# A gated attention block on one core: norm factors in x, sums of products in PSUM, merges and two gates among the units

## The chip, the core and the metric

One core of a Trainium2 chip runs the whole program once. The metric is the device time of one execution in microseconds (us). The engines are TensorE (PE: products, with PEld for loading its weights), VectorE (DVE), ScalarE (ACT), GpSimd (POOL) and SyncE (SP), whose queue issues the DMA transfers. Each engine takes its instructions strictly in the order in which the program lists them, and waits on semaphores for the others. SBUF is the working memory of the engines; PSUM, in eight banks of 128 x 512 numbers, takes the results of PE.

## The reference

x is 2048 tokens by 1024. In short:

```
h = rms_norm(x) * norm_gain
proj = h @ w_in                     # 1024 x 8448
q, k, v of A (8 heads, 2 kv heads), q, k, v of B (3 groups of 8 heads), ga, gb (512 each), mg (2 x 1024)
ya = windowed attention of A * silu(ga)
yb = softmax-merge over the 3 groups of the dilated attentions of B * silu(gb)
merged = sigmoid(mg0 + b0) * (ya @ w_branch_a) + sigmoid(mg1 + b1) * (yb @ w_branch_b)
out = x + merged @ w_out
```

q and k get a norm per head, and both branches a relative-position bias.

## The kernel before

Every float32 operand of a product is split into a high and a low float16 part, and a product is three: high with high, low with high, high with low. The weights are scaled by a power of two first, found from their sum of squares.

**Prologue.** Sixteen tiles of x (128 tokens) are loaded (x_load, line 437), squared on ACT for the norm (x_square), scaled by the norm factor on DVE (x_scale, 471), turned by PE (x_turn, 475) and split into XH and XL (x_hi, x_lo), which stay in SBUF. The gain of the norm is not in x: it is multiplied into every weight tile on POOL (gains, 182; w_gain, 187; g_gain, 334) ahead of the square (w_square, 220) that the scale comes from (w_sum, 230, a product with ones on PE, line 199; w_pow on DVE). Once four tiles of x are there, PE computes the silu gates of chunks 0 and 1 of 128 columns directly (g_step, 368): 24 products of 512 columns for each quarter of the tokens.

**Units.** Fourteen units (unit_order, 48): A0, B of head pair 0 with dilation 4, A1, then the others of B. Each unit has eight steps; a step projects two blocks of 128 tokens (Pair, 641: 48 products of 384 columns, line 657) while the attention of earlier blocks goes on (Item, 773): logits on PE (825), bias and maximum on DVE (860), exponents and split on ACT and DVE (868, 873, 877), a transposing DMA of p (883), the values (894), and a store to DRAM (zd for B, za for A). An A unit has 32 such items, a B unit 16. The order of all instructions is written out as a plan: `at(t, f)` puts f at time t, in steps, into a heap, and the lists in capitals at the top hold the offsets. Between the products of the units stand other pieces of work: loads and scales of the next unit's weights, and the squares of weights of later stages. A dictionary `fill` lists gates that are computed directly within given steps; before, it holds only pair 0 (mg_step, 1117), in four steps of two gates behind the last unit.

**Gate stage.** The other gates come in pairs of 128 columns each (PAIRS, 62; "m" for merge gates, "s" for silu gates). Pair 1 is computed directly for two quarters of the tokens (gate_pair, 1363). Then come halves (gate_group, 1423): a block product of 2 x 2 blocks in seven instead of eight products (the scheme of Strassen and Winograd), each of twelve matmuls (line 1441). It needs sums of blocks of x (x_sums, 1398: POOL adds on line 1406, DVE on 410 and 1413, ACT on 1409; four chunks for each of two halves of the tokens) and sums of weights (w_sums, 1086: POOL 1109, ACT 1110, DVE 1104). Each of the seven products has a PSUM bank of its own (`fps`, eight banks); ACT copies (1446), DVE additions (1449) and POOL additions (1452) join them; then come tanh on ACT (1350, 1359), for silu a product on DVE (1360), and a store to DRAM. In 19 halves each pair's weights are prepared (prep, 1371) while the pair ahead is computed.

In the same stage lie the merges: eight of A (a_merge, 977) and sixteen of B (b_merge_q, 1011), each for one quarter of the tokens. A merge loads what the units stored, forms the factors of the softmax in small DVE and ACT operations (988 to 1000; 1026 to 1039), multiplies on POOL (1005; 1043) and, for B, adds on DVE (1047, 1048). Its result, y, goes straight into a YPart (921): four transposes by PE (939), the product with the silu gate (942), a maximum (946) and a store to ytd; after the fourth quarter a sum over the partitions by PE (max2, 959, the matmul on line 199).

**Branch and output stages.** The products of y with the branch weights (branch_pair, 1592, line 320) are gated, merged on POOL, split again and multiplied by w_out (group, 1671, line 1667).

Of the kernel before, what the change touches and what calls it, by code (L numbers as in the profile page):

```python
# [40 lines left out]
SX = 2.0 ** 10  # L41
# [21 lines left out]
PAIRS[2:2], PAIRS[0:0] = [("s", 4), ("s", 6)], [("s", 2)]  # L63

V_ONES = 0.077
EVAC = (0.015, 0.025, 0.099)
NORM = (0.028, 0.136, 0.32, 0.626, 0.744, 0.904, 0.962, 1.033, 1.118)
LS = 2.887
LAGS = {'A': (-0.21, 0.002, 0.019, 0.144, 0.276, 0.337, 0.417), 'B': (-0.156, -0.001, 0.042, 0.169, 0.19, 0.379, 0.525)}
LV = {'A': 1.111, 'B': 1.829}  # L70
OUT = 0.007
DRAIN = 0.8
A_MERGE = (4.588, 5.306, 7.494, 7.578, 10.432, 1.944)
B_MERGE = (4.5, 5.692, 7.721, 9.584, 10.41, 10.858, 13.0, 2.546)
Y_PART = (-4.492, 1.142, 1.179, 2.058, 2.995)
GATE = (-0.1, -0.064, 0.329)
W_STEP = (0.1, 0.465, 1.9, 0.445, 4.197, 0.146, 0.342)
W_MAX = (3.762, 3.892)
N_PREP = (5.9, 6.3, 7.15, 7.753)
B_GAP = (0.25, 0.138, 0.231)  # L80
W_LAST = 1.9
T_SUM = (3.065, 4.03)
Y_MAX = (1.0, 3.749, 2.734)
X_SQ = (5.098, 1.401, 9.779, 2.051)
X_CH = (9.3, 2.65, 1.024, 0.955, 1.155, 1.305)
X_ST = (1.3, 0.179)
X_G = (7.5, 15.282, 45.87)
X_GP = (2.1, 5.694, 7.094, 7.694, 8.894, 10.194)
# [3 lines left out]
T_Y = (2.0, 0.8, 1.897, 1.5, 4.347, 26.0, 0.5, 1.3, 2.282, 1.289, 2.066)  # L92
T_P = (3.726, 15.7, 4.2, 8.277, 5.649)
T_X = (0.5, 25.538, 5.083)
T_Z = (66.0, 8.5, 10.8, 11.961, 4.431)
T_O = (0.5, 11.195, 25.513, 29.616, 59.0, 67.057)
T_G = (-54.762, -17.359, -13.9, -13.5)
T_S = (0.0, 0.0, 1.45, 1.512, 1.132, 2.442, 1.723, 1.505, 0.8, 1.857)
T_H = (-20.666, 0.693, 0.178)
T_GATE = (0.1, -0.19, 0.735, 1.0, 2.8)  # L100
T_W = (5.5, 1.621, 8.634, 1.493, 15.16, 15.823, 0.472, 0.8, 1.345)
T_B = (20.984, 6.5, 1.55, 0.725)
T_BR = (7.513, 0.071, 21.94, 8.769, 39.063)
T_A = (0.3, 0.262, 1.5, 0.8, 1.2)
T_M = (16.0, 14.0, 2.0, 2.0, 1.097)
# [11 lines left out]
def block_kernel(tc, x, w_units, w_gate, w_mrg, w_brn, w_out, w_bra, gain, qkg, sink, bias_a, bias_b, b_merge, out):  # L117
# [34 lines left out]
    gn = cst.tile([128, NCH], F32, name="gn")  # L152
# [28 lines left out]

    def gains(raw, c0, n):

        v = raw[:, c0:c0 + 2, :n]
        G.tensor_tensor(v, v, gn[:, c0:c0 + 2].unsqueeze(2).to_broadcast([128, 2, n]), OP.mult)  # L185

    def w_gain(u, i):
        gains(wtiles[u][0], 2 * i, 384 if u < NU else 256)

# [1610 lines left out]
```

## Time and profile before

| | |
|---|---|
| median of three runs | 2061.72 us (2061.12 to 2063.66) |
| profiled execution | 2062.36 us |
| its span, first to last instruction | 2060.6 us |
| mean granted PE clock | 0.982 |
| busy: PE, DVE, ACT, POOL | 1922.8, 1488.7, 1099.2, 1084.6 us |

Busy times are of the whole span and hide that stages have different limits. So they are to be read by stretches: the prediction cuts the span where PE's products change from one line of the kernel to the next. A row of such a view names the stretch, its length, then for each engine its busy time with the number of instructions, the granted clock of PE (1.00 is full speed), the mean share of time in which the sixteen DMA engines were busy, and GB/s. Rows of waits name the instruction that waited, what released it, and total, number and longest of the waits in us. Rows of one line give minimum, median and maximum duration in ns.

### The profile page before, as it was taken

The page shows a single profiled execution, that of the slowest core. Times are in us where ns is not written, and L with a number is a line of the kernel's source. Part 1 is how long each engine was busy: PE and PEld are TensorE (multiplying, and loading weights), DVE is VectorE, ACT ScalarE, POOL GpSimd, SP SyncE. Part 2 cuts the span into 40 slices and gives each one's busy share as a digit, 9 for nine tenths or more (in the row PEclk, how much of TensorE's full clock was granted, in tenths as well). Part 3 has the DMA queues.
Part 4 walks back from the last instruction along what each step waited for, and adds up shares of the span by engine and source line. Part 5 has one row for each costly group of instructions (what it writes and reads, how often), then busy time and mean ns, then how long its engine had stood idle before and what let it go on. Part 6 is the DMA issues. An engine that isn't in the chain of part 4 may idle for free. (4 is left out here: it accounts for less than half of the span.)

```text
span 2060.6 us, 40879 instructions
## 1 busy us (share of the span) xinstructions
PE 1922.8 (93%) x13700; PEld 1202.9 (58%) x13700; DVE 1488.7 (72%) x3478; ACT 1099.2 (53%) x2493; POOL 1084.6 (53%) x2460
## 2 busy tenths in 40 slices
PE   8989999999999999999999997778889899999999
PEld 5566666786678667876788653233344444434444
DVE  6588769867677677667776657978888877787522
ACT  7477668766666666666666653353333335442200
POOL 4254565556656656656665636755566541123434
PEclk9999999999999999999999999889999999999999
DMA  5269779975876786866775661145556555779764
GB/s 228 81 116 198 128 155 159 196 142 112 173 151 121 142 164 116 165 143 122 156 149 100 122 146 62 46 160 178 162 166 191 168 174 162 234 227 283 238 233 154
DMA packets 625460, 325.71 MB, mean 158 GB/s; under 512 B 462688, under 2 KB 565472, under 8 KB 623968
## 3 DMA queue, kind: packets, MB, share of 16 engines
q1 hardware_dynamic: 625248, 323.10, 64.8%
q8 instruction: 107, 1.75, 0.4%
q14 instruction: 105, 0.86, 0.2%
HBM read 138.56 MB, written 73.92 MB: 103 GB/s over the span
## 5 line engine op out<-in xcount | busy, mean ns | idle before, releaser
L657 PE MATMUL pj<-wh,XH 128*128 128x384 f16 x1792 | 585.2, 327 | 3.6 <-DVE vt L697 3.4
L657 PE MATMUL pj<-wh,XL 128*128 128x384 f16 x1792 | 586.5, 327 | 0.0
L657 PE MATMUL pj<-wl,XH 128*128 128x384 f16 x1792 | 585.0, 326 | 0.0
L657 PEld LDWEIGHTS <-XH 128*128 128x128 f16 x3584 | 411.9, 116 | 148.1 <-issue 5.8
L868 ACT ACTIVATE pr<-pr,z 128x256 f32<-128x256 f32 (+3 forms) x512 | 226.2, 494 | 37.2 <-DVE z L860 37.0
L657 PEld LDWEIGHTS <-XL 128*128 128x128 f16 x1792 | 207.5, 116 | 64.2 <-issue 0.3
L860 DVE CUSTOM_DVE_ANT_0 pr<-s,b,ubuf 128x256 f32<-128x256 f32 (+3 forms) x512 | 218.4, 463 | 30.2 <-PE s L825 27.6
L721 DVE TENSOR_TENSOR rw<-rw,qr 128x512 f32<-128x512 f32 (+1 forms) x112 | 112.2, 1002 | 141.1 <-POOL vt L684 118.9
L877 DVE SCALAR_TENSOR_TENSOR p<-pr,p 128x512 f16<-128x512 f32 (+2 forms) x256 | 185.6, 725 | 24.9 <-ACT p L873 22.4
L728 POOL TENSOR_TENSOR rw<-rw,g 128x128 f32<-128x128 f32 (+1 forms) x224 | 149.0, 684 | 90.0 <-DVE rw L721 84.8
L743 POOL COPY spl<-spl 128x256 f16<-128x256 f16 (+1 forms) x224 | 85.5, 411 | 169.9 <-DVE spl L738 168.5
L873 ACT ACTIVATE p<-pr 128x512 f16<-128x512 f32 (+2 forms) x256 | 159.5, 623 | 25.1 <-DMA pt<-p 16.7
L734 ACT ACTIVATE spl<-rw 128x512 f16<-128x512 f32 (+1 forms) x112 | 72.1, 644 | 185.9 <-POOL vt L684 162.8
L825 PE MATMUL s<-kq 128*128 128x256 f16 (+3 forms) x1328 | 149.6, 243 | 21.6 <-DMA kq<-spl 16.3
L281 POOL TENSOR_TENSOR rs_t<-rs_y 128x8 f32<-128x8 f32 (+2 forms) x345 | 91.1, 264 | 143.6 <-DVE rs_y L272 119.2
L320 PE MATMUL fps<-Y,wh 128*128 128x512 f16 x512 | 154.2, 382 | 6.8 <-DVE kp L1600 3.6
L894 PEld LDWEIGHTS <-pt 128*128 128x128 f16 x3024 | 124.1, 97 | 49.7 <-DMA pt<-p 22.2
L894 PE MATMUL pv<-vt,pt 128*128 128x65 f16 (+1 forms) x2784 | 132.0, 193 | 15.3 <-DMA pt<-p 15.2
L1667 PE MATMUL fps<-wt,M 128*128 128x512 f16 (+1 forms) x684 | 145.2, 375 | 0.0
L825 PEld LDWEIGHTS <-kq 128*128 128x128 f16 x1328 | 109.8, 98 | 59.5 <-DMA kq<-spl 17.4
L185 POOL TENSOR_TENSOR wraw<-wraw,gn 128x768 f32<-128x768 f32 (+1 forms) x100 | 136.6, 1374 | 0.3 <-DMA wraw<-in_w_mrg_dram 0.3
L1441 PEld LDWEIGHTS <-wh 128*128 128x128 f16 x760 | 76.9, 102 | 91.2 <-issue 11.0
(226 smaller groups left out, 3799.5 us busy)
## 6 DMA issues: line engine op xcount, KB each, us to landing
wraw<-in_w_units_dram SPq DMA_DIRECT2D x56, 384.0 KB, 4.4
mgd<-fg SPq DMA_DIRECT2D x64, 256.0 KB, 2.4
mtd<-mm SPq DMA_DIRECT2D x56, 256.0 KB, 3.2
M<-mtd SPq DMA_DIRECT2D x8, 1792.0 KB, 9.5
zd<-z SPq DMA_DIRECT2D x192, 66.0 KB, 1.9
Y<-zd SPq DMA_DIRECT2D x48, 264.0 KB, 4.2
wraw<-in_w_mrg_dram SPq DMA_DIRECT2D x44, 256.0 KB, 4.0
xt<-in_x_dram SPq DMA_DIRECT2D x16, 512.0 KB, 8.8
```

Of the source, the lines that this page charges most:

```text
L185: G.tensor_tensor(v, v, gn[:, c0:c0 + 2].unsqueeze(2).to_broadcast([128, 2, n]), OP.mult)
L320: out.append(lambda w=w, xx=xx, ch=ch, i=i: T.matmul(ps[:], lhsT=w[:, ch, c0:c0 + 128], rhs=xx[:, ch, ts], start=(i == 0), stop=(i == n - 1)))
L657: out.append(lambda lhs=lhs, rhs=rhs, ch=ch, k=k: T.matmul(ps[:, :384], lhsT=lhs[:, ch, :], rhs=rhs[:, ch, :384], start=(k == 0), stop=(k ...
L721: V.tensor_tensor(q, q, self.rr[:, :n].unsqueeze(2).to_broadcast([128, n, HD]), OP.mult)
L728: G.tensor_tensor(q[:, i, :un.nq, :], q[:, i, :un.nq, :], g, OP.mult)
L825: T.matmul(self.sv[j][:, o:o + w], lhsT=q[0][:, h, q[1]:q[1] + 128], rhs=kt[:, kh + v * un.nk, k0:k0 + w], start=(v == 0), stop=(v == 1))
L860: V.tensor_tensor_reduce(out=self.pv[:, j, self.p0:self.p0 + W], in0=self.sv[j], in1=un.bias[:, self.h0 + j, self.b0:self.b0 + W], scale=I ...
L868: A.activation(v, v, AF.Exp, bias=self.stat(j), scale=-1.0)
L873: A.activation(self.sp[:, :128 * n], self.pr, AF.Copy, scale=PSC)
L877: V.scalar_tensor_tensor(self.sp[:, 128 * n:], self.pr, PSC, self.sp[:, :128 * n], OP.mult, OP.subtract)
L894: T.matmul(self.po[:, j, :w], lhsT=p[:, n * j + s, :], rhs=un.v[key][:, vh, c0:c0 + w], start=(k == 0 and s == 0), stop=(k == 2 and s == n ...
L1667: mm.append(lambda ch=ch, k=k, w=w, i=i: T.matmul(ps[:, :cols.stop - cols.start], lhsT=m[:, a, ch, k, :], rhs=wt[w][:, b, ch, cols], start ...
```

## The change

Four things change together.

1. The gain of the norm is loaded once, broadcast to 128 partitions (gr), scaled by a power of two (gain_scale), and multiplied into x by x_scale, which becomes an operation on two tensors. All POOL multiplications of weights by the gain are removed; the constant scale SX becomes a value found at run time (sx, isx, ihx).
2. A half of a pair keeps its seven products in three PSUM banks: U1 = A11 B11 is copied out, S2 T2 is added on top of it in the same bank, which is copied out again, then S3 T3 and A22 N4; S4 B22 is added on top of S1 T1. The sums of x lose their factor of a quarter, and the POOL additions go. The last gate reads its sum from PSUM.
3. The merges of A and of B's head pairs 0 to 2 move into the units, at steps 25.4 to 31 and 33.1 to 39 (A), and from steps 44.8, 68.8 and 92.8 on (B). They use a buffer of their own (zz, one copy) and store y to DRAM (yd) by two transfers for each chunk. The YParts stay in the gate stage, 7.12 us apart, and load y from there. Pair 3 of B is merged in the gate stage as before.
4. The list of pairs loses the silu pair of chunks 2 and 3. These two chunks are computed directly, one gate in each of steps 1, 3, 5, 7 (in A0) and 17, 19, 21, 23 (in A1). The merge pair of chunk 3 takes the direct place behind the units. The gate stage has 17 halves.

The many other constants are offsets of the plan. The core of the diff:

```diff
-SX = 2.0 ** 10
+SX = 2.0 ** 9
...
-PAIRS[2:2], PAIRS[0:0] = [("s", 4), ("s", 6)], [("s", 2)]
-
...
+MERGES = (25.362, 1.5, 33.1, 1.639, 44.848, 2.916)
...
+A_MERGE = (0.705, 0.964, 0.937, 0.95, 1.1, 1.13, 0.986)
+B_MERGE = (0.5, 0.65, 0.712, 0.456, 1.15, 1.031, 1.725, 1.5, 1.879)
+Y_PART = (-4.658, 1.142, 1.254, 2.446, 2.904)
+A_FILL = ((1, 3, 5, 7), (17, 19, 21, 23))
+X_GAIN = 6.588
-T_Z = (66.0, 8.5, 10.8, 11.961, 4.431)
+T_Z = (52.0, 7.12, 13.638, 4.085, 5.0)
...
-    def gains(raw, c0, n):
-
-        v = raw[:, c0:c0 + 2, :n]
-        G.tensor_tensor(v, v, gn[:, c0:c0 + 2].unsqueeze(2).to_broadcast([128, 2, n]), OP.mult)
-
-    def w_gain(u, i):
-        gains(wtiles[u][0], 2 * i, 384 if u < NU else 256)
...
+    gr = sp0.tile([128, D], F32, name="gr")
+
+    def gain_scale():
+        m = sm.tile([128, 1], F32, name="gm")
+        V.tensor_reduce(m[:], gr[:], AX.X, OP.max, apply_absolute_value=True)
+        s, i = pow2(m[:], "x")
+        V.tensor_scalar(sx[:], s[:], SX * 2.0 ** -15, None, OP.mult)
+        V.tensor_scalar(isx[:], i[:], 2.0 ** 15 / SX, None, OP.mult)
+        V.tensor_scalar(ihx[:], isx[:], 0.5, None, OP.mult)
+        V.tensor_scalar(gr[:], gr[:], s[:], 2.0 ** -15, OP.mult, OP.mult)
+        done.add("gain")
...
-        V.tensor_scalar(xts[t][:], xts[t][:], xss[groups[t]][:, i:i + 1], None, OP.mult)
+        assert "gain" in done and ("sq", t) in done
+        V.scalar_tensor_tensor(xts[t][:], xts[t][:], xss[groups[t]][:, i:i + 1], gr[:], OP.mult, OP.mult)
...
+    at(X_G[0] + X_GP[5] + .1, g_load, 2)
+    for c in range(3):
         b = X_G[c]
-        chain([(b + X_GP[0] * i, g_gain, c, i) for i in range(2)]
-              + [(b + d, f, c) for d, f in zip(X_GP[1:], (g_square, g_sum, g_pow, g_hi, g_lo))])
+        chain(in_turn(b, X_GP[1:], [(f, c) for f in (g_square, g_sum, g_pow, g_hi, g_lo)]))
     at(X_W[0], w_load, 0)
...
-        def __init__(self, chunk, q, y, o):
-            self.chunk, self.q, self.y, self.o = chunk, q, y, o
+        def __init__(self, chunk, q):
+            self.chunk, self.q = chunk, q
         def load(self):
-            assert ("gt", self.chunk, self.q) in done
-            nc.sync.dma_start(out=self.o, in_=gtd[self.chunk][:, 512 * self.q:512 * self.q + 512])
+            c, q = self.chunk, self.q
+            assert ("gt", c, q) in done and ("yd", c, q) in done
+            self.y, self.o = spare(), spare()
+            nc.sync.dma_start(out=self.y.rearrange("p (b f) -> p b f", b=4),
+                              in_=yd[c][512 * q:512 * q + 512, :].rearrange("(b p) f -> p b f", p=128))
+            nc.sync.dma_start(out=self.o, in_=gtd[c][:, 512 * q:512 * q + 512])
         def plan(self, t):
...
+    def y_keep(c, q, v):
+        d = yd[c][512 * q:512 * q + 512, :].rearrange("(b p) (h e) -> p b h e", p=128, h=2)
+        for h in range(2):
+            nc.sync.dma_start(out=d[:, :, h, :], in_=v[:, :, h, :])
+        done.add(("yd", c, q))
+
     def a_merge(t, j, q):
-        nhalf[0] += 1
...
         def product(c):
-            y = spare().rearrange("p (b h e) -> p b h e", b=4, e=HD)
             hs = slice(2 * c, 2 * c + 2)
-            G.tensor_tensor(y, z[:, :, hs, 0:HD], e1[:, :, hs].unsqueeze(3).to_broadcast([128, 4, 2, HD]), OP.mult)
-            YPart(2 * j + c, q, y.rearrange("p b h e -> p b (h e)"), spare()).plan(now[0] + A_MERGE[5])
-
-        for b, f, *args in in_turn(t, A_MERGE, (exponents, exps, factors), [(product, c) for c in range(2)]):
+            v = z[:, :, hs, 0:HD]
+            G.tensor_tensor(v, v, e1[:, :, hs].unsqueeze(3).to_broadcast([128, 4, 2, HD]), OP.mult)
+
+        def keep(c):
+            y_keep(2 * j + c, q, z[:, :, 2 * c:2 * c + 2, 0:HD])
+
+        for b, f, *args in in_turn(t, A_MERGE, (exponents, exps, factors), [(product, c) for c in range(2)], [(keep, c) for c in range(2)]):
...
-        def sums():
-            y = spare().rearrange("p (b h e) -> p b h e", b=4, e=HD)
-            V.tensor_tensor(y, zz[:, 0, :, :, 0:HD], zz[:, 1, :, :, 0:HD], OP.add)
-            V.tensor_tensor(y, y, zz[:, 2, :, :, 0:HD], OP.add)
-            YPart(4 + j, q, y.rearrange("p b h e -> p b (h e)"), spare()).plan(now[0] + B_MERGE[7])
-
-        for b, f, *args in in_turn(t, B_MERGE, (exponents, exps, factors), [(product, g) for g in range(3)], (sums,)):
+        def sums(g):
+            y = zz[:, 0, :, :, 0:HD]
+            V.tensor_tensor(y, y, zz[:, g, :, :, 0:HD], OP.add)
+
+        def keep():
+            y_keep(4 + j, q, zz[:, 0, :, :, 0:HD])
+
+        for b, f, *args in in_turn(t, times, (exponents, exps, factors), [(product, g) for g in range(3)],
+                                   [(sums, 1), (sums, 2)], (keep,)):
             at(b, f, *args)
+
+    def zz_tile():
+        return wk.tile([128, 1584], F32, name="zz", bufs=1)[:]
...
+            if ("w", NU + n) not in done:
+                return False
...
-        return tproj_list(ps, wtiles[NU][3], wtiles[NU][4], 128 * k, q), gate_steps(ps, PAIRS[0][1] + k, q, imh, None)
+        return tproj_list(ps, wtiles[NU][3], wtiles[NU][4], 128 * k, q), gate_steps(ps, None, q, imh, 2 * PAIRS[0][1] + k)
...
+        for j in range(2):
+            b = MERGES[2 * j] + MERGES[2 * j + 1] * q
+            at(b, a_merge, b, j, q)
+        for j in range(3):
+            b = MERGES[4] + 24 * j + MERGES[5] * q
+            at(b, b_merge_q, b, j, q, zz_tile, B_MERGE)
+    for q in range(4):
         fill.setdefault(NPAIR + q, []).extend((mg_step, q, k) for k in range(2))
+        for c in range(2):
+            fill.setdefault(A_FILL[c][q], []).append((g_step, 2 + c, q))
...
-            A.activation(xsum(b, c, p)[0], v, AF.Copy, scale=0.25)
+            A.activation(xsum(b, c, p)[0], v, AF.Copy)
         def lo(v, b):
             h, l = xsum(b, c, p)
-            V.scalar_tensor_tensor(l, v, 0.25, h, OP.mult, OP.subtract)
+            V.tensor_tensor(l, v, h, OP.subtract)
             done.add(("xs", b, c, p))
...
-        def products(ps, x, bl):
+        def products(ps, x, bl, first, last):
             mm = []
             for ch in range(4):
                 for k, w in ((0, 0), (1, 0), (0, 1)):
                     i = len(mm)
                     mm.append(lambda ch=ch, k=k, w=w, i=i: T.matmul(
-                        ps[:], lhsT=weight(bl, ch)[w], rhs=xblock(x, ch, p)[k], start=(i == 0), stop=(i == 11)))
+                        ps[:], lhsT=weight(bl, ch)[w], rhs=xblock(x, ch, p)[k], start=bool(first and i == 0), stop=(i == 11), skip_group_check=True))
             return mm
-        def copy(o, ps, scale):
-            A.activation(o, ps[:], AF.Copy, scale=scale)
-
-        def plus(o, ps, v, scale):
-            V.scalar_tensor_tensor(o, ps[:], scale, v, OP.mult, OP.add)
-
-        def add(o, x, y):
-            G.tensor_tensor(o, x, y, OP.add)
-
-        def gate(o, k, q, late):
-            gate_out(n, k, q + p, o, o, now[0] + late)
-
-        def two(ps):
-            d = tile_()
-            plus(d, ps, a, 1.0)
-            gate(d, 0, 0, T_S[8])
-
-        steps = ((A11, B11, lambda ps: copy(a, ps, 1.0)), (A12, B21, two), (S1, T1, lambda ps: copy(b, ps, 16.0)),
-                 (S2, T2, lambda ps: (plus(c, ps, a, 16.0), add(a, b, c))),
-                 (S3, T3, lambda ps: (plus(c, ps, c, 16.0), add(b, b, c), gate(b, 1, 2, T_S[9]))),
-                 (S4, B22, lambda ps: (plus(a, ps, a, 4.0), gate(a, 1, 0, T_S[8]))),
-                 (A22, N4, lambda ps: (plus(c, ps, c, 4.0), gate(c, 0, 2, T_S[8]))))
-        for k, (x, bl, f) in enumerate(steps):
-            if k == 0:
-                a = tile_()
-            if k == 2:
-                b, c = tile_(), tile_()
-            ps = ps_p.tile([128, 512], F32, name="fps")
-            at(job(2.6, products(ps, x, bl)) + T_GATE[0], f, ps)
+        def keep(k, ps):
+            v[k] = tile_()
+            A.activation(v[k], ps[:], AF.Copy)
+
+        def plus(k, ps, col, q):
+            V.tensor_tensor(v[k], ps[:], v[k], OP.add)
+            gate_out(n, col, q + p, v[k], v[k], now[0] + T_S[8])
+
+        def direct(ps):
+            gate_out(n, 0, 2 + p, ps[:], tile_(), now[0])
+
+        v, banks = {}, {}
+        steps = (("a", A11, B11, 1, 0, lambda ps: keep(0, ps)), ("b", A12, B21, 1, 1, lambda ps: plus(0, ps, 0, 0)),
+                 ("a", S2, T2, 0, 0, lambda ps: keep(1, ps)), ("c", S1, T1, 1, 0, lambda ps: keep(2, ps)),
+                 ("a", S3, T3, 0, 0, lambda ps: plus(2, ps, 1, 2)), ("c", S4, B22, 0, 1, lambda ps: plus(1, ps, 1, 0)),
+                 ("a", A22, N4, 0, 1, direct))
+        for bank, x, bl, first, last, f in steps:
+            if first:
+                banks[bank] = ps_p.tile([128, 512], F32, name="fps")
+            ps = banks[bank]
+            at(job(2.6, products(ps, x, bl, first, last)) + T_GATE[0], f, ps)
...
-    order_ += [("s", n, p) for n in range(3, 9) for p in range(2)] + [("s", 9, 1), ("s", 10, 1), ("s", 9, 0), ("s", 10, 0)]
+    order_ += [("s", n, p) for n in range(3, 8) for p in range(2)] + [("s", 8, 1), ("s", 9, 1), ("s", 8, 0), ("s", 9, 0)]
...
+        b = m + T_Z[2] * q
+        at(b, b_merge_q, b, 3, q, lambda q=q: half(q % 2), B_TAIL)
+    for c in range(8):
+        for q in range(4):
+            at(m, lambda c=c, q=q: YPart(c, q).plan(now[0] - Y_PART[0]))
+            m += T_Z[1]
+    chain([(m + T_Z[3], y_scales)])
     for j in range(2):
```

More of the change, by code (lines that the diff above doesn't have):

```diff
@@ L424, in chain, with in_turn @@
             at(e[0], go, k)
+    def in_turn(t, times, *groups):
+        steps, b = [], 0
+        for d, f in zip(times, [f for g in groups for f in g]):
+            b = max(b, t + d)
+            steps.append((b, *f) if isinstance(f, tuple) else (b, f))
+            b += .001
+        return steps
     st = ExitStack()
@@ L517, in block_kernel @@
         at(.01 * t, x_load, t)
-    at(.015, lambda: nc.sync.dma_start(out=gn[:], in_=gain))
+    at(.015, lambda: nc.sync.dma_start(out=gr[:], in_=gain.broadcast_to([128, D])))
+    at(X_GAIN, gain_scale)
     at(.035, g_load, 0)
@@ L668, in plan @@
             steps = (self.square, self.stats, self.newton, self.scale, self.gain, self.hi, self.lo, self.swap, self.turn)
-            for d, f in zip(NORM, steps):
-                at(e[1] + d, f)
+            for b, f in in_turn(e[1], NORM, steps):
+                at(b, f)
         def evac_qk(self, i):
```

167 lines of the change are left out of this document (73 added, 94 removed).

## The prediction

> **What bounds the kernel now.** I read busy times by stretch first, cut where the products of TensorE (PE) change their line; then whom PE waited for in the critical stretches; then single lines. The execution took 2062.36 us: its span and 1.76 us around it.
>
> ```profile
> span 2060.6 us, 40879 instructions
> core 0: us, PE busy (x) PEld busy (x) DVE busy (x) ACT busy (x) POOL busy (x), PEclk, DMA share, GB/s
> 0.00:80.10 80.10, 70.58 (x410) 44.39 (x411) 55.34 (x132) 51.98 (x90) 26.02 (x56) 0.98 0.43 163
> 80.10:1201.60 1121.50, 1081.03 (x9635) 802.79 (x9634) 815.90 (x2255) 745.44 (x1861) 660.63 (x2092) 1.00 0.75 144
> 1251.20:1366.30 115.10, 81.69 (x350) 35.42 (x351) 105.08 (x115) 49.17 (x86) 83.64 (x55) 0.87 0.17 58
> 1366.30:1734.00 367.70, 326.53 (x1505) 153.36 (x1504) 305.78 (x658) 142.27 (x268) 189.70 (x151) 0.95 0.55 175
> ```
>
> Prologue, fourteen units and, after 49.6 us of direct gates, the gate stage in two parts (482.8 us). In the units PE is nearly always busy. At the start of the gate stage VectorE (DVE) is: 105 of 115 us, while PE has 82 and a granted clock of 0.87.
>
> What should PE need there? The output stage runs without such waits, so its products give the price:
>
> ```profile
> L1667 PE MATMUL fps<-wt,M x684: 272/379/380, 1912.1 to 2057.1; 128*128 128x512 f16 x165, 128*128 128x256 f16 x6
> ```
>
> 145 us for 672 products of 512 columns (24 of the 684 are halves): 0.216 us each, 2.59 for twelve, 18.1 for one half of a pair (seven times twelve), 5.2 for a direct gate of 24. The gate stage holds 19 halves and four direct gates, 365 us; it takes 118 more. In it PE waits:
>
> ```profile
> PE fps L199 <- ACT XL L228: 26.6, 2, 16.4
> PE fps L1441 <- DVE yq L1104: 4.3, 1, 4.3
> ...
> PE fps L939 <- DVE wt L1048: 16.3, 6, 5.0
> PE fps L939 <- POOL wt L1005: 13.0, 6, 4.8
> PE fps L199 <- DVE ym L957: 6.3, 3, 2.3
> PE fps L939 <- DVE ubuf L1340: 3.1, 1, 3.1
> ```
>
> The columns are total, times, longest. The first two lines are of the first part, the others of the second; lines under 3 us (6.5 together) are left out, and the sum is 76. L199 sums squares of weights, which ScalarE (ACT) could take only after the gain on GpSimd (POOL). L939 turns merged y: it waits for the merges. The other 42 us:
>
> ```profile
> 1372.52 0.60 PE L939 MATMUL fps<-idf,wt 128*128 128x128 f32 x4
> 1372.96 0.38 PE L1441 MATMUL fps<-XH,wl 128*128 128x512 f16 x1
> L199 PE MATMUL fps<-wsq,ones x18: 169/253/376, 1286.2 to 1646.0; 128*128 128x4 f32 x18
> ```
>
> A turn of four transposes takes 0.44 us from start to start, 32 of them 14; 17 sums at 0.25 take 4. The remaining 24 I put down to the lowered clock after waits: 0.3 us for each us waited.
>
> **The change, part by part.** *Two silu chunks become direct gates.* The list has one pair less, a merge pair takes the direct place behind the units, and two chunks of A are computed inside units A0 and A1. The gate stage loses two halves, 36.2 us; 329 us of products stay. The units gain 8 gates of 5.2, 41.4 us. Only PE's idle time can hide them:
>
> ```profile
> 80.10:171.10 91.00, 84.80 (x790) 56.43 (x789) 67.82 (x159) 59.14 (x125) 45.95 (x128) 1.00 0.66 129
> 171.10:229.60 58.50, 51.30 (x586) 38.51 (x583) 47.55 (x116) 41.87 (x94) 27.76 (x79) 0.97 0.96 183
> 266.40:362.60 96.20, 89.79 (x932) 62.22 (x931) 79.91 (x200) 72.26 (x160) 55.45 (x154) 1.00 0.83 158
> 528.00:604.70 76.70, 74.94 (x656) 55.28 (x654) 55.43 (x152) 51.40 (x128) 48.24 (x154) 1.00 0.78 148
> ```
>
> A0 and A1 (first and third row) leave 12.6 us; the half unit behind A0 (second) leaves 7, with a DMA share of 0.96, but no gate goes there. I let half of the 12.6 hide: +35 (+29 if all hides, +41 if none). Each gate's tanh, product and store, some 0.7 us on ACT and on DVE (like L1449 below), lie beside PE there.
>
> *The gain goes into x.* 100 POOL products go, each ahead of a square:
>
> ```profile
> L185 POOL TENSOR_TENSOR wraw<-wraw,gn x100: 1032/1466/2272, 47.3 to 1640.2; 128x768 f32<-128x768 f32 x56, 128x512 f32<-128x512 f32 x44
> L1406 POOL TENSOR_TENSOR Y<-XH,XL x32: 1153/1596/1601, 1252.3 to 1336.3; 128x512 f32<-128x512 f16 x32
> L410 DVE TENSOR_TENSOR Y<-Y x32: 674/1399/1749, 1256.3 to 1343.9; 128x512 f32<-128x512 f32 x32
> L1449 DVE SCALAR_TENSOR_TENSOR fg<-fps,fg x95: 672/681/693, 1297.0 to 1738.0; 128x512 f32<-128x512 f32 x95
> ```
>
> The minimum, median and maximum say it: beside POOL a DVE operation on two SBUF operands takes 1.4 us or more instead of 0.67; with one operand in PSUM (L1449) it stays at 0.68. So the sums over x (64 such operations on DVE, 32 on POOL) bind the first part: the two take turns, 64 x 0.65 + 32 x 1.0 = 74 us by estimate. Eight gains and six adds of POOL there go, about 1 us of DVE's time each, and nine of the L1449, 6 us: 20 of the 105 us. The sums themselves stay, and PE wants them as early as before; they are late next. Of the 35 us waited in the first part I keep 15 (bounds 5 and 35).
>
> In the prologue the scaling of x becomes an operation on two tensors, and 512 KB of broadcast gains are loaded ahead of most tiles:
>
> ```profile
> L473 DVE TENSOR_SCALAR xt<-xt,xr x16: 735/746/1484, 9.1 to 62.2; 128x1024 f32<-128x1024 f32 x16
> L365 DVE SCALAR_TENSOR_TENSOR gl<-graw,ubuf,gh x2: 1276/1277/1278, 22.1 to 33.1; 128x1024 f16<-128x1024 f32 x2
> xt<-in_x_dram SPq DMA_DIRECT2D x16, 512.0 KB, 8.8
> ```
>
> That is 16 x (1.28 - 0.75) = 8.5 us on DVE, which is busy 55 of 80 us. PE's gates hide what comes after the first tiles, and POOL's gains ahead of gate 0 go. +1.5; bounds -2 and one landing, +8.8.
>
> *Merges into the units.* Eight merges of A and twelve of B leave the gate stage; four of B stay, and all 32 turns, each with one more load.
>
> ```profile
> L1035 DVE TENSOR_TENSOR bm_s<-bm_d 128x8 f32<-128x8 f32 x16 | 7.0, 438 | 0.5
> L1037 DVE RECIPROCAL bm_s<-bm_s 128x8 f32<-128x8 f32 x16 | 3.2, 203 | 0.5
> L1047 DVE TENSOR_TENSOR wt<-Y x16: 677/1516/1750, 1473.0 to 1676.6; 128x512 f32<-128x512 f32 x16
> L1043 POOL TENSOR_TENSOR Y<-Y,bm_e x48: 1034/1049/1492, 1470.5 to 1676.5; 128x512 f32<-128x512 f32 x48
> Y<-zd SPq DMA_DIRECT2D x48, 264.0 KB, 4.2
> wt<-gtd SPq DMA_DIRECT2D x32, 256.0 KB, 4.4
> ```
>
> A B merge has ten small DVE operations between 0.2 and 0.44 us, some 2.9 together, two sums of 1.4 and three POOL products: 5.7 us and 3.2. An A merge, with seven small ones and two products, takes about 2 and 2.4. DVE gains 84 us in the units on top of 816, 80% of the time, still below PE; POOL gains 58 and loses 56 gains, 82. The cost is one of order. SyncE's (SP) queue takes three loads and two stores per B merge, one and four per A merge; a store waits for the sums, and behind it stand the transposes of k, q and p. DVE's first small operation stands half a step (4.8 us by the row of 528 to 604.7, eight steps) behind three loads that land 4.2 us after issue. Where they are late, the evacuation of v waits behind it, with the other product's 24 x 0.162 = 3.9 us as cover.
>
> ```profile
> PE s L825 <- DMA kq<-spl: 16.3, 16, 2.1
> PE pj L657 <- DVE vt L697: 3.4, 6, 1.8
> ```
>
> These are waits in all units. I take 0.4 us a merge, +8, nearest to the second row (0.6 each); bounds 0 and 3 us, +60. A lighter POOL shortens the way to k and q: -3 of the first row (bounds 0 and -8).
>
> In the gate stage the turn now waits for a load put 5.8 us ahead that lands in 4.4, not for a merge: of L939's 34 us I keep 4, of L199's ym 6 (bounds 2 and 41 together).
>
> *Sums in PSUM.* Seven products share three banks instead of seven. Five DVE operations, two ACT copies and two POOL adds become two, three and none; the last gate reads PSUM. New: at four places a half, a read must end before PE goes on in that bank, with one other product, 2.59 us, in between.
>
> ```profile
> L1350 ACT ACTIVATE fg<-fg,bmh,ubuf 128x512 f32<-128x512 f32 x48 | 38.4, 811 | 107.0 <-POOL fg L1452 70.2 <-DVE ubuf L1340 15.4 <-DVE fg L1449 15.2
> L1446 ACT ACTIVATE fg<-fps 128x512 f32<-128x512 f32 x32 | 18.6, 581 | 7.5 <-PE fps L1441 6.6 <-ACT wt L1283 0.4 <-ACT fg L1350 0.4
> ```
>
> A copy takes 0.58 us, so two ACT operations may stand ahead of it unseen. No row shows such a wait: 0 at best, and at worst, with a tanh (0.81) that itself waits for DVE, 1.5 us each. I take 0.12, 8 us for 68 reads: ACT is busy 142 of 368 us, and the tanh's longest releaser, POOL's add, is gone.
>
> **The sum.** Waits left in the gate stage: 15 + 10 + 8 = 33, with their clock 43. With products 329, turns 14, sums 4 it lasts 390 instead of 483: -92. Units +35 + 8 - 3 = +40. Prologue +1.5. Direct gates, branch and output keep their work. 2062.4 - 51 = 2012, and by the median of the runs, 2061.7, **2011 us**.
>
> **Rivals.** *The gate stage at its floor*: 5 us of waits instead of 33 give 354 us there, and 1975 in all. For: DVE and POOL lose much of their load. Against: the sums over x stay where they are.
>
> *Merges hold PE in the units*: at 2 us each 32 us more, 2043. For: DVE, ACT and SP run in order, and the DMA share is 0.96 behind A0. Against: PE is at work 1081 of 1121 us, and waits little for DVE. The Trainium skill (DMA: Bandwidth & Descriptors, Specifications) asks for 512 B or more for line rate; the merged y is stored in runs of 256 B, and no row here has such a store.
>
> *Slower, by the reads between*: 68 reads, each holding PE once ACT or DVE is over 2.59 us late. From 0.7 us each (51 / 1.3 / 68, and the 0.12 counted) nothing is gained; at 1 us they cost 88 instead of 10: 2089. For: ACT's tanh still waits for DVE (15 us above), and a copy behind it waits too. Against: both engines lose work. The Trainium skill (PSUM — Partial Sum Buffer, PSUM bank collisions raise a hardware error) has a bank guarded as a whole, so that no read could overlap with the next product in its bank. No run here shows that yet.
>
> **Chances.** Forecast 0.45 (1990 to 2030), floor 0.22, merges 0.20, reads 0.13. Range 1963 to 2052: it leaves out the reads and the far end of the floor. A measurement of this kernel tells about 0.2% from no change: faster 0.85, same 0.02, slower 0.13.
>
> **What would show it.** A gate stage near 390 us, few waits of L939, a clock near 1. Product waits there on ACT copies or DVE sums are the reads. Units near 1161 us: steps with gates 5 us longer is the fill, new waits on k, q or v the merges. A prologue of some 82 us. I am wrong if the first part still waits 30 us and more: then the sums over x alone set it.

## The result and the profile after

Four runs took 2036.25 us in the median (2031.33 to 2043.09), against 2061.42 us of the kernel before in the same job. The ratio is 0.9879, 95% interval 0.9848 to 0.991: faster by 1.2%, 25 us where 51 were forecast. The profiled execution took 2034.54 us, with a span of 2032.8. The windows below are cut where PE's products change their line; first of the kernel after, then of the kernel before (prologue, units, direct gates, gate stage, branch products, output).

```profile
core 0: us, PE busy (x) PEld busy (x) DVE busy (x) ACT busy (x) POOL busy (x), PEclk, DMA share, GB/s
0.00:84.20 84.20, 70.09 (x412) 44.89 (x413) 65.21 (x150) 53.75 (x93) 18.72 (x49) 0.92 0.44 168
84.20:1276.60 1192.40, 1129.60 (x9842) 826.74 (x9841) 835.41 (x2473) 767.41 (x1901) 639.45 (x2086) 0.99 0.80 156
1276.60:1325.00 48.40, 47.53 (x340) 24.65 (x339) 18.14 (x49) 26.19 (x57) 11.54 (x24) 1.00 0.56 115
1325.00:1715.40 390.40, 358.14 (x1685) 170.09 (x1685) 281.00 (x508) 183.29 (x318) 111.87 (x76) 0.97 0.52 163
1715.40:1884.10 168.70, 166.48 (x770) 75.02 (x769) 135.43 (x196) 64.43 (x102) 45.58 (x30) 1.00 0.80 251
1884.10:2032.80 148.70, 145.37 (x685) 66.82 (x683) 47.25 (x62) 17.77 (x26) 65.67 (x50) 1.00 0.61 211
```
```profile
1251.20:1734.00 482.80, 408.22 (x1854) 188.78 (x1855) 410.87 (x771) 191.44 (x353) 273.34 (x206) 0.93 0.46 147
1734.00:1912.10 178.10, 169.75 (x770) 75.07 (x769) 137.23 (x201) 66.70 (x106) 47.07 (x31) 0.99 0.77 241
```

Stage by stage: prologue +4 (forecast +1.5), **units +71 (forecast +40)**, direct gates -1, **gate stage -92 (forecast -92)**, branch products -9 (forecast 0), output 0. The gain arrived where it was expected; the units gave back more than was counted. Whom PE waited for in the units (total, times, longest):

```profile
PE pv L912 <- DMA pt<-p: 27.7, 23, 2.9
PE s L843 <- DMA kq<-spl: 19.1, 15, 3.5
PE pj L675 <- DVE vt L715: 15.1, 17, 1.9
```

62 us with a rest of 0.5, against 40 before. The transposes of p, and of k and q, come late, and so does v. In the 40 of the kernel before, two rows stand beside the two that the prediction shows:

```profile
PE pv L894 <- DMA pt<-p: 15.2, 14, 2.1
PE s L825 <- DVE z L860: 5.2, 8, 0.9
```

In the gate stage of the kernel after:

```profile
PE fps L1473 <- ACT fg L1479: 20.0, 6, 7.8
PE fps L952 <- DMA wt<-yd: 4.1, 3, 1.9
PE fps L1473 <- DVE fg L1482: 3.2, 2, 2.9
PE fps L952 <- DVE bm_e L1046: 2.9, 1, 2.9
PE fps L196 <- ACT XL L225: 2.1, 1, 2.1
```

With 0.9 at the start that is 33 us, as forecast. L1479 is the ACT copy and L1482 the DVE sum that read PSUM between products.

### The profile page after: what moved, and what is told of

Read it like the earlier page. It is cut to its first block, busy times and chain, and to the rows that moved or that the text cites. A ratio compares the mean times of both kernels' runs of the same rounds, so it can differ in the third digit from the quotient of the medians.

```text
span 2032.8 us, 40777 instructions
## 1 busy us (share of the span) xinstructions
PE 1917.2 (94%) x13726; PEld 1208.2 (59%) x13726; DVE 1382.4 (68%) x3435; ACT 1112.8 (55%) x2496; POOL 892.8 (44%) x2314
## 4 chain that ended last, share of the span: by engine, by line
PE 63%; DMA 11%; DVE 10%; POOL 7%; issue 5%; ACT 3%; SPq 1%; POOLq 0%; DVEq 0%; ACTq 0%
PE pj L675 23%; PE fps L1473 11%; PE fps L1690 7%; PE fps L317 7%; PE pj L317 6%; PE s L843 4%; DMA pt<-p 4%; PE pv L912 3%; DMA kq<-spl 2%; DMA zz<-zd 2%; DVE Y L404 2%; POOL rs_t L277 1%; POOL rw L746 1%; POOL rs_t L278 1%; DVE qss L727 1%
## 5 line engine op out<-in xcount | busy, mean ns | idle before, releaser
L675 PE MATMUL pj<-wh,XH 128*128 128x384 f16 x1792 | 588.4, 328 | 15.1 <-DVE vt L715 15.1
L675 PEld LDWEIGHTS <-XH 128*128 128x128 f16 x3584 | 396.9, 117 | 161.8 <-issue 20.1
L895 DVE SCALAR_TENSOR_TENSOR p<-pr,p 128x512 f16<-128x512 f32 (+2 forms) x256 | 179.1, 700 | 29.2 <-ACT p L891 27.6
L746 POOL TENSOR_TENSOR rw<-rw,g 128x128 f32<-128x128 f32 (+1 forms) x224 | 139.2, 641 | 129.4 <-DVE rw L739 125.4
L843 PE MATMUL s<-kq 128*128 128x256 f16 (+3 forms) x1328 | 148.5, 244 | 19.3 <-DMA kq<-spl 19.1
L277 POOL TENSOR_TENSOR rs_t<-rs_y 128x8 f32<-128x8 f32 (+2 forms) x345 | 100.3, 291 | 131.7 <-DVE rs_y L268 110.6
L739 DVE TENSOR_TENSOR rw<-rw,qr 128x512 f32<-128x512 f32 (+1 forms) x112 | 85.5, 763 | 106.2 <-POOL vt L702 77.8
L916 ACT ACTIVATE z<-pv 128x130 f32<-128x130 f32 x256 | 69.6, 272 | 143.8 <-PE pv L912 142.7
L694 ACT ACTIVATE rw<-pj 128x256 f32<-128x256 f32 (+1 forms) x224 | 87.1, 389 | 110.6 <-PE pj L675 109.5
L756 DVE TENSOR_TENSOR spl<-rw,spl 128x512 f16<-128x512 f32 (+1 forms) x112 | 83.6, 747 | 88.0 <-ACT spl L752 87.8
```

The costliest lines, as they stand in the source:

```text
L277: G.tensor_tensor(tv, yv, yv, OP.mult)
L675: out.append(lambda lhs=lhs, rhs=rhs, ch=ch, k=k: T.matmul(ps[:, :384], lhsT=lhs[:, ch, :], rhs=rhs[:, ch, :384], start=(k == 0), stop=(k ...
L746: G.tensor_tensor(q[:, i, :un.nq, :], q[:, i, :un.nq, :], g, OP.mult)
L843: T.matmul(self.sv[j][:, o:o + w], lhsT=q[0][:, h, q[1]:q[1] + 128], rhs=kt[:, kh + v * un.nk, k0:k0 + w], start=(v == 0), stop=(v == 1))
L895: V.scalar_tensor_tensor(self.sp[:, 128 * n:], self.pr, PSC, self.sp[:, :128 * n], OP.mult, OP.subtract)
```

## The experiments

All are edits of the changed kernel, shown shortened. Ratios are to the kernel before. Stages are those of one profiled execution; the units of kernels with the same work there differed by 3 to 4 us (1133.5 in e1 and 1130.7 in e15; 1192.4 in the changed kernel, 1191.4 in e9 and 1188.2 in e12), so a difference of that size shows nothing. B02 is the unit of B's head pair 0 and group 2, and so on. I began with theory 1: DVE stands at a merge's first small operation until the merge's load has landed, and v's evacuation stands behind it. In its favour, the kernel after, from the first merge to the end of the units:

```profile
DVE am_n L1005 <- DMA zz<-za: 17.3, 7, 3.2
DVE bm_n L1045 <- DMA zz<-zd: 8.7, 10, 1.9
DVE bm_n L1044 <- DMA zz<-zd: 6.1, 5, 2.0
```

### Where the units' 71 us come from: e1, e2, e3, e4

```diff
 e1 -            at(b, a_merge, b, j, q)                       (units)
    +            at(m, a_merge, m, j, q); m += 7.4             (gate stage; b_merge_q alike, m += 9.5)
    offsets in a merge as before the change; the YParts start at t + 66 instead of t + 52
 e2 e1, and
    -A_FILL = ((1, 3, 5, 7), (17, 19, 21, 23))
    +A_FILL = ((NPAIR + 4, NPAIR + 5, NPAIR + 6, NPAIR + 7),) * 2
 e3 every time in A_MERGE and B_MERGE + 0.35; MERGES pitch of A 1.9
 e4 +            if work or f is keep:      (only the loads and the stores of a merge)
```

> The eight merges of A and twelve of B leave the units and stand in the gate stage again, in the half tiles, at 7.4 and 9.5 steps of its clock; the turns stay apart, with their loads and stores. Theory 1 (in the units DVE's first small operation of a merge waits for the landing of its load, and POOL's products and SP's stores stand ahead of the work for k, q and p; together some 46 us): units 1192 to about 1146 us, gate stage 390 to about 415 because the merges' DVE work comes back beside it, in all about 2016. Rival A (the gates that fill A0 and A1 carry the extra time, the merges little): units 1180 or more, in all 2045 or more.

> As the kernel with the merges back, and the eight gates of the two chunks stand behind the units instead of in A0 and A1. Against that kernel: theory 1 (about 16 of the fill's 41 us hide in idle time of PE in A0 and A1): units 25 us shorter, direct gates 41 us longer, in all 16 us more. Rival A (the fill hides nothing or disturbs): units 40 us shorter or more, in all the same or less.

> Every step of a merge in the units behind its load stands 0.35 of a step (about 3.3 us) later, and A's merges stand 1.9 steps apart instead of 1.5 and 1.64, so that their tile is free in time. Theory 1 (the landing is what DVE waits for): DVE's waits for the merge tile fall from 32 us to under 8, units 20 to 30 us shorter, in all 2006 to 2016. Rival B (the price is the traffic and the places in SP's and POOL's queues, not the landing): the waits for the tile fall too, but the units stay within 5 us of 1192.

> The twenty merges in the units keep their loads and stores, and leave out the arithmetic on DVE, ACT and POOL between them, so the merged values are not the reference's. Theory 1: with nothing that waits for the landing but the stores, units 35 to 46 us shorter, 1146 to 1157. Rival B (traffic and SP's order): units at most 10 us shorter, 1182 or more.

Measured: e1 2028.22 us, ratio 0.9844 (0.9828 to 0.9861). e2 2026.7 us, 0.9844 (0.9828 to 0.986). e3 2034.24 us, 0.9874 (0.9857 to 0.989). e4 2000.44 us, 0.9712 (0.9694 to 0.9729). The windows, first the units and then the gate stage of e1, and units, direct gates and gate stage of e2:

```profile
84.60:1218.10 1133.50, 1117.84 (x9842) 825.91 (x9841) 774.24 (x2273) 763.98 (x1873) 569.75 (x2034) 1.00 0.77 145
1266.50:1708.70 442.20, 377.07 (x1684) 173.94 (x1684) 337.22 (x708) 187.49 (x346) 171.12 (x128) 0.93 0.64 192
```
```profile
83.90:1184.50 1100.60, 1077.91 (x9649) 806.76 (x9648) 765.76 (x2265) 756.39 (x1865) 573.48 (x2035) 1.00 0.79 148
1184.50:1275.00 90.50, 89.00 (x533) 43.48 (x531) 24.45 (x60) 33.02 (x67) 20.29 (x31) 1.00 0.35 85
1275.00:1708.90 433.90, 374.08 (x1684) 173.42 (x1684) 330.16 (x707) 185.51 (x344) 159.46 (x120) 0.94 0.65 196
```

e1's units fell further than theory 1 said (1133.5, not 1146), and its gate stage grew more (442, not 415). e2's units and e4's came out between their two expectations (33 and 31 us shorter).

Read as a ledger the rows close: 1121.6 us before; 1100.6 with neither merges nor fill (-21); 1133.5 with the fill (+33); 1192.4 with the merges (+59). The merges cost 2.95 us each there, and took 52 us off the gate stage (442.2 to 390.4): **the move is no gain**. By these stages it loses some 7 us; the medians, 2036 and 2028, say the same, but the intervals overlap, so a loss isn't shown. In e1's units PE waited 15 us instead of 62:

```profile
PE pv L912 <- DMA pt<-p: 10.2, 9, 2.3
PE s L843 <- DMA kq<-spl: 4.4, 8, 0.9
PE pj L675 <- DVE vt L715: 0.8, 1, 0.8
```

That is 47 of the 59 us. The other 12 are in PE's busy time (1129.6 and 1117.8 us), with a granted clock of 0.99 instead of 1.00. The fill costs the units 33 us of its 42 (90.5 less 48.4 behind the units), and with the gates behind them the gate stage is 8 us shorter: no difference in all.

e3 fells theory 1. Its DVE hardly waits for the merge tile any more:

```profile
DVE bm_n L1045 <- DMA zz<-zd: 0.2, 1, 0.2
```
```profile
85.10:1278.50 1193.40, 1133.12 (x9842) 828.65 (x9841) 848.79 (x2473) 768.12 (x1901) 634.94 (x2086) 0.99 0.80 156
```

The waits of 17.3, 8.7 and 6.1 us fell to 0.2, and the units stayed at 1193. DVE waited elsewhere instead (for POOL's vt at L739 87.7 us, 73.3 in the changed kernel), and PE's waits stayed (28.5, 17.4 and 13.2 for p, for k and q, and for v). So taking these waits away gained nothing. e4 splits the price instead: loads and stores alone 28 us (1161.4 less 1133.5), arithmetic 31.

### Which part of a merge costs: e5, e6, e7, e17

```diff
 e5 -MERGES = (25.362, 1.5, 33.1, 1.639, 44.848, 2.916)
    +MERGES = (56.2, 1.9, 80.2, 1.9, 44.848, 2.916)
 e6 +            G.tensor_tensor(out[c]..., v, ...)     (out: free columns of the tile, side by side)
    -        for h in range(2):
    -            nc.sync.dma_start(out=d[:, :, h, :], in_=v[:, :, h, :])
    +        nc.sync.dma_start(out=yd[c][512 * q:512 * q + 512, :]..., in_=v...)
 e7 +            if work or f is not product:
 e17 e6 with two transfers of 256 rows instead of one of 512
```

> A's eight merges leave B02 and B00 (DMA share 0.93 and 0.86 with them) and stand 1.9 steps apart in B10 and B20, which have no load of a merge and a share of 0.73 and 0.77. Theory 2 (a merge costs by its traffic where the queues are full already): B02 and B00 lose 20 us or more together, B10 and B20 gain under 10, units 1192 to about 1178, in all about 2022. Rival C (a merge costs some 3 us wherever it stands): B10 and B20 gain 20 to 25, units 1187 to 1197.

> The merged y is written side by side before the store (A's products into free columns of the merge tile, B's second sum into those of its second group), and goes out as one transfer with runs of 512 B instead of two with runs of 256 B. If the short runs and the second transfer are much of the 28 us that loads and stores alone cost: units 10 to 20 us shorter. If it is the loads, or the places in SP's queue: at most 5 us.

> The 52 products of merges on POOL in the units are left out (so the merged values are not the reference's), everything else of the merges stays: small operations and sums on DVE, loads and stores. Arithmetic costs 31 us in the units. If POOL's products carry it (they stand ahead of the norms of q and k on POOL, and DVE runs slower beside them): units 20 to 30 us shorter. If DVE's own operations carry it: at most 10 us.

> As the run with stores of 512 B, but each merged block goes out as two transfers of half the rows, as many transfers as in the changed kernel, with runs of 512 B. If the run length gave the 15 us in the units: they stay within 4 of 1177. If the second transfer in SP's queue did: 1187 to 1193.

Measured: e5 2023.05 us, 0.981 (0.978 to 0.984). e6 2020.47, 0.9805 (0.978 to 0.9829). e7 2015.79, 0.9779 (0.9753 to 0.9806). e17 2032.36, 0.9856 (0.984 to 0.9872). Units of e6, e7 and e17:

```profile
85.50:1262.90 1177.40, 1126.02 (x9841) 825.08 (x9840) 835.37 (x2473) 767.14 (x1901) 638.34 (x2086) 1.00 0.82 158
```
```profile
83.90:1253.40 1169.50, 1123.47 (x9842) 825.00 (x9841) 816.36 (x2473) 768.11 (x1901) 575.15 (x2034) 1.00 0.82 159
```
```profile
83.80:1274.50 1190.70, 1130.41 (x9841) 826.95 (x9840) 836.17 (x2473) 767.74 (x1901) 641.38 (x2086) 0.99 0.80 156
```

e7: POOL's 52 products carry 23 us, which leaves, by difference, 8 of the 31 for the small operations and sums on DVE and ACT. How the products cost isn't settled: without them PE waits for v 5.3 us instead of 15.1, for k and q 14.5 instead of 19.1, and DVE's 2473 operations take 816 us instead of 835. So DVE running slower beside POOL may be as much of the cause as POOL's order. e6: one transfer instead of two makes the units 15 us shorter. e17 tells which half of that edit did it: with runs of 512 B and as many transfers as in the changed kernel they take 1190.7, as with runs of 256 B (1192.4). **The number of transfers costs, not the length of the runs.** PE's waits for the transposes of p, k and q agree: 46.8 us in the changed kernel, 47.4 in e17, 37.3 in e6. The rule of 512 B that the prediction set beside this rival (the Trainium skill, DMA: Bandwidth & Descriptors, Specifications) showed no effect here.

What a transfer takes in SP's queue stands in SP's timeline of the changed kernel (start, us, line, transfers in the row):

```profile
533.53 1.24 SPq L901 DMA_TRANSPOSE pt<-p  x1
534.87 2.29 SPq L993 DMA_DIRECT2D yd<-zz  x4
537.25 0.48 SPq L926 DMA_DIRECT2D zd<-z  x1
537.82 3.82 SPq L767 DMA_TRANSPOSE kq<-spl  x3
541.75 1.25 SPq L901 DMA_TRANSPOSE pt<-p  x1
543.10 1.72 SPq L999 DMA_DIRECT2D zz<-za  x1
```

A store of y takes 0.57 us of the queue here, a transpose 1.2 or more, and in this stretch the rows stand end to end. A row of several transfers includes the time between them; transfer by transfer, SP's issues take 883 of 1122 us in the units before the change, 945 of 1192 after it and 924 of 1177 in e6. In the rest SP mostly waits, in order, for others: for DVE's p alone (L901) 78 us after the change. The 28 transfers fewer are 16 us by such rows (28 x 0.57), and the units got 15 shorter (13 against e17). The page of the profile does not count issuing as busy, so none of this shows in its first part.

e5's units are 12 us shorter (1180.4), between its two expectations: B02 and B00 lost 27 us, and B10 and B20 took 22 back; the other 7 are spread over ten units. An A merge costs nearly the same where the DMA share is low, so traffic alone isn't its price.

### Better versions, and the queue: e10, e13, e14, e15, e18

```diff
 e10 e5 + e6      e13 e6, MERGES = (56.2, 3.15, 80.2, 3.15, 44.848, 2.916)
 e14 e6, a_merge in the gate stage      e15 e6, all merges in the gate stage
 e18 e6, and for weights of the next unit, branch pieces and the merge tile
 -nc.sync.dma_start(
 +nc.scalar.dma_start(
```

> The two edits that made the units shorter together: A's merges in B10 and B20 (12 us by themselves) and stores of 512 B (15 us). If they act at different places: units about 1165, in all 2007 to 2012. If both only relieve B02 and B00: units 1172 to 1177, in all 2016 to 2021.

> As the run with light units and 512 B, with A's merges 3.15 steps apart (over B10 and the half of B21 behind it, over B20 and the half of B31 behind it) instead of 1.9. There each A merge still cost about 3 us, while B's, 2.9 steps apart, cost about 2. If the distance sets the price: units 1178.6 to 1165 to 1172. If an A merge costs its 3 us (two transfers out, two products) wherever it is: 1176 to 1181.

> Only A's eight merges go back into the gate stage; B's twelve stay in the units, all stores of 512 B. Against the run with stores of 512 B (units 1177, gate stage 391): units lose the 20 us of B02 and B00, about 1157; the gate stage gains 10 to 20, since an A merge has 2 us of DVE's work; in all 2010 to 2016. If merges cost the gate stage 2.6 us each, as all twenty did: 2020.

> All merges back in the gate stage, with stores of 512 B. Against the first run with the merges back (2028 us, gate stage 442): if the short stores cost the gate stage anything, it gets 5 to 15 us shorter; if DVE's and POOL's work is what costs there, it stays within 3 of 442.

> As the run with stores of 512 B, and 128 loads that wait for little (weights of the next unit, pieces of the branch weights, the merge tile) are issued by ACT instead of SP in the units. SP's own rows fill 1040 of the 1177 us there, 0.5 us a plain transfer and 1.4 a transpose; with 28 fewer transfers the units were 15 us shorter, with as many of double length they were not. If SP's queue is the second bound of the units: some 64 us of it go, units 1140 to 1160, in all about 1995. If SP is full only because it waits in order for others: units 1170 or more, and ACT's issues delay its own work.

Measured: e10 2017.26 us, 0.9796 (0.9781 to 0.981). e13 2022.97, 0.9811 (0.9794 to 0.9827). e14 2021.72, 0.9803 (0.9787 to 0.982). e15 2025.06, 0.9812 (0.9798 to 0.9827). e18 2063.62, 1.0028 (1.0005 to 1.005).

e10 is the fastest of the complete kernels, 2.0% under the kernel before, but its interval overlaps e6's, and the two edits don't add: its units take 1178.6, no less than e6's, where its expectations had 1165 and 1172 to 1177. e13's take 1178.3: the distance between merges is not the price. e14 shows what A's merges are worth: units 18 us less, gate stage 20 more, so 2022 in all and not the 2010 to 2016 of its first expectation. In e15 the units take 1130.7 and the gate stage 442.3, as in e1: there the number of stores costs nothing, and with the cheaper stores the move of all merges is even in all (0.9812 in e15, 0.9805 in e6).

e18 refuted its first expectation (1140 to 1160) and met the second (1170 or more), far beyond its bound. (The 1040 us for SP's rows in its text are too many; transfer by transfer it is 924.) SP's issues fell from 924 to 882 us, and the units grew by 40 against e6. The view shows the units first, then whom PE waited for in them:

```profile
85.80:1303.00 1217.20, 1142.19 (x9841) 831.58 (x9840) 840.23 (x2473) 767.42 (x1901) 638.31 (x2086) 0.98 0.80 153
```
```profile
PE pv L912 <- DMA pt<-p: 44.1, 27, 4.7
PE s L843 <- DMA kq<-spl: 18.8, 16, 3.6
```

The wait for p's transposes is 19 us longer than in e6 (25.4), though SP issued less. ACT makes p, and its exponentials now stand behind 128 issues of 0.33 us or more each; that these carry the 40 us is a reading, not shown. The Trainium skill (Trainium Kernel Development and Optimization, Key Constraints) says that issuing from several engines saves only the sequencer's issue time; here SP's was saved and more was lost. So it stays open whether SP's queue is itself a bound of the units. Shown is only that 28 stores fewer in it made the units 13 to 15 us shorter, about the 0.5 us each that they take in it.

### The other 21 us of the units: e8, e11, e16

```diff
 e8  e1, and ahead of w_square, on POOL
 +        G.tensor_tensor(v, v, gn[...] (ones), OP.mult)
 e11 e2, with V_ONES, EVAC, NORM, LAGS and LV from before the change      e16 e11 + e8's product
```

> The kernel with the merges back, and on POOL ahead of each square of weights in the units a product with ones, as the gain was before (56 products of 384 columns or 256). With merges and fill both back the units took 1100.6 us, 21 less than before the change. If the lighter POOL gave that: units 1133 to about 1150 to 1156. If the new due times of the steps gave it: units at most 5 us longer.

> The kernel with merges and fill both back (units 1100.6 us), with the due times from before the change for what a unit issues on DVE, ACT and POOL: evacuations, norms, exponentials, values. The gains on POOL explained 7 of the 21 us by which its units are shorter than before the change. If the new due times gave the rest: units 1112 to 1118. If not: 1103 or less.

> Merges and fill both back, the due times from before the change, and products with ones on POOL for the gains: in the units nearly the work and order of the kernel before (1121.6 us). Old due times alone gave 1104.7, the gains alone some 7 us more. If the two add: 1110 to 1114, and 8 to 12 us stay open. If they work on each other (a later q and k behind the gains meets an earlier due time): 1117 to 1123, and the account of the units closes.

Measured: e8 2033.22 us, 0.9866 (0.9841 to 0.9891). e11 2034.74, 0.9881 (0.9865 to 0.9898). e16 2053.45, 0.9953 (0.9939 to 0.9968). Units of e8, e11 and e16:

```profile
84.20:1224.90 1140.70, 1120.21 (x9842) 826.63 (x9841) 811.32 (x2272) 764.47 (x1873) 649.92 (x2090) 1.00 0.76 144
```
```profile
85.50:1190.20 1104.70, 1077.73 (x9638) 803.10 (x9637) 783.56 (x2264) 751.09 (x1866) 580.55 (x2035) 1.00 0.78 147
```
```profile
84.00:1206.30 1122.30, 1083.77 (x9637) 804.57 (x9636) 818.35 (x2264) 746.18 (x1864) 663.01 (x2091) 1.00 0.77 145
```

With new due times the gains cost 7 us (1140.7 less 1133.5, between e8's expectations), with old ones 18 (1122.3 less 1104.7). Old due times without gains cost 4, no more than the scatter. Both together give 1122.3, the 1121.6 of the kernel before: the account closes. That the two work on each other is likely but not shown, since e8 has the fill in A0 and A1 and e11 and e16 don't.

### Sums in PSUM and the prologue: e9, e12

```diff
 e9  -steps = (("a", A11, B11, 1, 0, lambda ps: keep(0, ps)), ...      (three banks)
     +steps = ((A11, B11, lambda ps: copy(a, ps, 1.0)), ...            (seven, as before)
 e12 -V.scalar_tensor_tensor(xts[t][:], xts[t][:], xss[...], gr[:], OP.mult, OP.mult)
     +V.tensor_scalar(xts[t][:], xts[t][:], xss[...], None, OP.mult)
```

> In the gate stage the sums of a half are made outside PSUM again, as before the change (seven banks a half; five DVE operations, two ACT copies, two POOL adds; nothing is read between products). In the changed kernel PE waits 23 of its 32 us there for the copies and sums between, nearly all in the first 65 us. If those reads are a cost of their own: they go, gate stage 360 to 375 us. If they only show where PE meets the sums over x on DVE, which hold ACT's copies too: PE waits for the sums themselves, and with 51 more DVE operations beside them the gate stage takes 390 to 420.

> The scaling of x in the prologue is the operation on one tensor again (the gain is left out of the computation); the broadcast gains are still loaded and scaled. If the operation on two tensors is what made the prologue 4 us longer: prologue 84.2 to about 81. If it is the 512 KB of gains ahead of the tiles and their scaling: 83 to 85.

Measured: e9 2048.84 us, 0.9949 (0.9934 to 0.9964); gate stage and branch products 399.2 and 175.1 us instead of 390.4 and 168.7. e12 2030.22 us, 0.986 (0.9846 to 0.9875); prologue 82.5 us, 83.8 to 86.2 in the other runs. In e9's gate stage PE waited for:

```profile
PE fps L196 <- ACT XL L225: 14.7, 3, 12.3
PE fps L952 <- DMA wt<-yd: 10.8, 3, 6.1
PE fps L1473 <- DVE yq L1127: 6.6, 1, 6.6
```

The 23 us of reads are gone, and PE waits more, 42 us in all: for squares that stand on ACT behind the same sums over x, for sums of weights on DVE, for turns. In its first 70 us PE gets further without the reads (241 products and 14.1 us of waits, against 206 and 17.6), but soon after, up to 85 us into the stage, it waits 12.3 in one piece for squares. So taking the reads away did not take away the waits behind the sums over x. The 9 us by which the stage is longer are no price of the reads by themselves, since e9 also brings back work: 34 DVE additions and 34 on POOL. (Its expectation has 51 on DVE, as the prediction has two DVE additions left in a half; the changed kernel has three, 51 in 17 halves against 85 in e9.) In the first 70 us of the changed kernel DVE (third of the busy times) has 68, and ACT waited for it (in the first 85 us):

```profile
1325.00:1395.00 70.00, 50.88 (x206) 21.49 (x206) 68.31 (x72) 31.74 (x55) 50.57 (x34) 0.88 0.15 52
```
```profile
ACT wt L1441 <- DVE Y L404: 22.5, 17, 3.7
ACT XH L1441 <- DVE Y L404: 14.4, 6, 5.8
```

## Why the prediction was right in sign and wrong in size

- **Gate stage, -92: right in sum, by luck in its terms.** The last sum over x starts on DVE 81 us into the stage. Up to there PE waited 23.9 us (15 forecast), behind it 2.3 for reads (8) and 7.0 for turns (10, with ym): 33 in all, as forecast, because the errors cancel. By the prediction's own sign, "Product waits there on ACT copies or DVE sums are the reads", the reads hold 23 of the 33. That most of these would come from the sums over x without the reads too, as the forecast has it ("The sums themselves stay, and PE wants them as early as before"), e9 makes likely and doesn't prove. The DVE additions of a half fell to three, not to two. Moving the merges out gave 52 of the 92 (e1).
- **The fill, +35: right.** 33 (e2).
- **The merges: the step that failed.** "I take 0.4 us a merge, +8, nearest to the second row (0.6 each)": 59, the upper end of the bounds. I took the price from PE's waits for v alone, and thought of them as DVE standing at a landing. Waits for v grew from 0.8 us without the merges (e1) to 15.1, and e3 shows that DVE's waits for the landing are not their cause. Most of the price is elsewhere: 28 us with loads and stores (half of it goes with half the stores), 23 with POOL's products, 8 with DVE's and ACT's small operations. PE's waits for p and for k and q grew from 15 us (e1) to 47, and the row for p, 15.2 us in the kernel before, is not among those that the prediction weighed. The prediction did count the transfers ("behind it stand the transposes of k, q and p"), but gave them no time. That the number of transfers costs is shown for 28 stores (e6 and e17); that they cost by their time in SP's queue is the nearest reading (16 us by the rows, 13 to 15 measured), and for the other loads and stores it stays open.
- **The lighter POOL, -3: too small.** It was -21 with the new due times; with the old ones the gains alone are 18 (e11, e16). Merges 51 over and relief 18 under the forecast leave, with the fill, the 31 us by which the units missed.
- **Prologue, +1.5: 4.** About 2 may be the scaling on two tensors (e12), which is hardly more than the spread of the other runs; the rest was not taken apart.
- **Branch products, 0: -9.** With seven banks 6 of them are back (e9). That DVE and POOL leave the gate stage with less behind is a reading, not shown.
- **Rivals.** "Merges hold PE at 2 us each" had the place right, and 2.95 was its size. "Slower, by the reads between" is refuted by the result itself: the reads hold PE 23 us in all, 0.3 each. The gate stage was far from its floor of 354.

## What to carry to other kernels

Work moved beside a busy engine isn't free just because every engine has idle time. Price every transfer by its time in the issuing queue and every operation by what stands behind it in order, at the nearest rows' upper end. A wait seen in the trace is a cause only once taking it away moves the end. When a move saves in one stage and costs in another, undo the move alone: here it gained nothing.

## What the runs showed that I had not expected

- In the median a plain transfer holds SP's queue 0.5 us and a transpose 1.2; 28 transfers fewer made the units 15 us shorter, and twice the run length did nothing (1190.7 and 1192.4).
- 128 loads issued from ACT instead of SP made the units 40 us longer (e18).
- 32 us of DVE's waits could be taken away without any gain (e3).
